# Norm gain before, norm root after: the S5 input projection of a hybrid layer on one Trainium2 core

## The chip, the cores and the metric

The kernel runs on one core of a Trainium2 chip. Its time is the device time of one execution in microseconds (us); a kernel's time is the median over its runs. A profiled execution lasts from the program's start to its end; its span, from the first to the last instruction, is a little shorter. The engines are named as in the profile: PE multiplies matrices (PEld is its loading of weights), DVE and ACT work elementwise, POOL helps them, and SP issues most of the transfers (DMAs). An engine works through its instructions in order: if one waits, everything behind it on that engine waits too.

## The reference

One layer of a trunk with 1024 channels and 1024 time steps. What matters here is its start:

```python
def rms_norm(x, g):
    y = xf * lax.rsqrt(jnp.mean(xf * xf, axis=-1, keepdims=True) + NORM_EPS)
    return y.astype(x.dtype) * g

h = rms_norm(x, norm_mix_pre[l])
proj = h @ w_in[l]
p_rwkv = proj[..., :N_RWKV_COLS]
u_s5 = proj[..., N_RWKV_COLS:N_RWKV_COLS + S5_WIDTH]      # 512 columns
gates = jax.nn.sigmoid(proj[..., N_RWKV_COLS + S5_WIDTH:] + b_gate[l])
# s5_branch: a diagonal complex state space over u_s5: b_bar = (exp(lam*dt) - 1) / lam * b,
# an associative scan over time, Re(c s) + d u, then gelu and a sigmoid gate
o_s5 = s5_branch(u_s5, s5_a_re[l], s5_a_im[l], ...)
```

The RWKV branch, the merge of both branches, the output projection and a gated MLP follow.

## The kernel before

Tiles are 128 channels by 512 time steps; a half (`th` 0 or 1) is one 512 of the 1024 time steps, and `k` counts the eight groups of 128 channels. A product in full precision is three matmuls (`mm3_steps`, L172 to L174): each operand is split into a rounded high part and the rest, and high×high, high×low and low×high are added in PSUM. So a weight tile `wf` becomes `wh` (ACT, L156) and `wl` (DVE, L157), and a normed tile `x` becomes `hh` (ACT, L226) and `hl` (`hsplit`, L227: for odd `k` on POOL, for even `k` on DVE).

The front of the kernel is written in `front_half`. `norm(th)` squares the eight tiles on ACT (L955), adds the squares in pairs on DVE (L956), sums each pair over channels with four matmuls of one column (`sumsq`, L245), takes the inverse root on DVE (L265, and L131 to L139), spreads it over the partitions with four transposes (`spread`, L271), copies it to SBUF as `rbc` (ACT, L964), and multiplies each tile in place by the norm's weight and the root (DVE, L967), after which it is split. `s5_in` then makes the S5 inputs: for each half, 8 k × 4 output tiles b × 3 matmuls, 96 in all, evicted by an ACT copy that reverses and permutes the time steps (L1073), stored to HBM (`US`) and loaded again in another order as `u8` (`load_u8`). After that `s5_setup` works the 32-column parameters of S5 out on DVE in some 115 small operations (L320 to L475).

From there two lanes run beside a filler. `s5_tables` (L508 to L575 on DVE, then `abs` and two sines on ACT, L576 to L578) makes the tables of one batch b of 8 groups; `s5_batch` multiplies `u8` by them (PE L598), rotates (DVE L600 to L602), scans (L605), rotates back (L607, L608; L608's is the last) and makes the batch's outputs (PE L613 to L615). The filler is the other columns of the input projection: `mix_in` (the RWKV columns, evicted on ACT L977 and shifted on DVE L978) and `gate_tiles` (evicted on ACT L1013, where a table of the activation may have to be loaded).

PE's order is written by hand. `drive` keeps a planned time `now`: each step of a lane names its cost and how long it must rest before its next step (`T_TAB0` before the first batch's tables come on PE, `T_TRIG`, `T_SCAN`), and matmuls of the filler are set in between to fill these rests. On the chip this order is fixed: PE waits at a step of S5 if its tables or scans aren't there, whatever stands behind it. The other engines' orders are set by the scheduler, by priority (`HPN` before `HP`) and the time at which it expects operands. Filler matmuls come out of four PSUM tiles (`gm`); an eviction that is late stops PE when the fifth is wanted.

At the start the `vecs` (norm weights, biases) and the constants `csts` are loaded on POOL's queue, the raw S5 parameters (`ls`, `lr`, `li`) on SP's (L314 to L316).

## Time and profile before

| | |
|---|---|
| median of 3 runs | 1551.08 us (1547.18 to 1552.98) |
| the profiled execution's own time | 1552.89 us |
| its span | 1551.1 us |
| mean granted PE clock | 0.972 |
| PE busy | 1460.4 us |
| DVE busy | 1081.2 us |
| ACT busy | 687.0 us |
| first S5 input matmul on PE | 25.57 us |
| first operation of the first S5 tables on DVE | 78.96 us |
| PE's matmuls of the first S5 outputs that need the scans (L614) | 144.15 us |

The page gives each engine's busy share. The waits on PE are listed by what ended them; the timeline gives a row's start in us from the span's start, its length, and in brackets the idle time before it. A row with x2 or x4 joins so many instructions.

### The profile page before, as it was taken

The page shows a single profiled execution, that of the slowest core. Times are in us where ns is not written, and L with a number is a line of the kernel's source. Part 1 is how long each engine was busy: PE and PEld are TensorE (multiplying, and loading weights), DVE is VectorE, ACT ScalarE, POOL GpSimd, SP SyncE. Part 2 cuts the span into 40 slices and gives each one's busy share as a digit, 9 for nine tenths or more (in the row PEclk, how much of TensorE's full clock was granted, in tenths as well). Part 3 has the DMA queues.
Part 4 walks back from the last instruction along what each step waited for, and adds up shares of the span by engine and source line. Part 5 has one row for each costly group of instructions (what it writes and reads, how often), then busy time and mean ns, then how long its engine had stood idle before and what let it go on. Part 6 is the DMA issues. An engine that isn't in the chain of part 4 may idle for free.

```text
span 1551.1 us, 24273 instructions
## 1 busy us (share of the span) xinstructions
PE 1460.4 (94%) x9332; PEld 1194.8 (77%) x9332; DVE 1081.2 (70%) x1733; ACT 687.0 (44%) x1069; POOL 161.1 (10%) x180
## 2 busy tenths in 40 slices
...
GB/s 208 41 203 118 93 127 100 196 115 113 153 44 107 153 190 143 144 69 94 255 245 161 153 144 137 103 82 82 82 84 88 87 82 203 334 149 134 241 59 108
DMA packets 131107, 210.45 MB, mean 136 GB/s; under 512 B 37696, under 2 KB 43840, under 8 KB 130992
## 3 DMA queue, kind: packets, MB, share of 16 engines
...
## 4 chain that ended last, share of the span: by engine, by line
PE 69%; DVE 12%; DMA 8%; issue 5%; ACT 4%; POOL 1%; SPq 0%; DVEq 0%; ACTq 0%; POOLq 0%
PE gm L172 8%; PE gm L173 8%; PE gm L174 7%; PE rp L1382 4%; PE rp L1383 4%; PE rp L1384 4%; DMA st<-in_w_down_dram 2%; PE mm L1383 2%; PE mm L1382 2%; PE mm L1384 2%; PE ch L172 2%; PE ch L173 2%; PE ch L174 2%; PE d L1557 2%; PE d L1556 2%
## 5 line engine op out<-in xcount | busy, mean ns | idle before, releaser
L172 PE MATMUL gm<-hh,wh 128*128 128x512 f32 x688 | 284.7, 414 | 14.2 <-DVE hl L1118 8.8
L173 PE MATMUL gm<-hl,wh 128*128 128x512 f32 x688 | 273.4, 397 | 0.2 <-DVE hl L227 0.2
L174 PE MATMUL gm<-hh,wl 128*128 128x512 f32 x656 | 260.0, 396 | 0.0
L157 DVE TENSOR_TENSOR wl<-wf,wh 128x512 fp32r<-128x512 f32 x175 | 123.1, 705 | 116.1 <-ACT wh L156 108.1
L156 ACT CAST wh<-wf 128x512 fp32r<-128x512 f32 x179 | 110.5, 619 | 209.6 <-PE gm L173 129.4
L172 PEld LDWEIGHTS gm<-hh,wh 128*128 128x128 f32 x688 | 132.2, 192 | 49.0 <-DVE hl L1118 10.9
L173 PEld LDWEIGHTS gm<-hl,wh 128*128 128x128 f32 x688 | 132.3, 192 | 26.3 <-issue 1.0
L174 PEld LDWEIGHTS gm<-hh,wl 128*128 128x128 f32 x656 | 125.6, 191 | 27.5
L1557 PE MATMUL d<-xl,wh 128*128 128x512 f32 x308 | 120.2, 390 | 3.5 <-DVE xl L227 3.5
L1556 PE MATMUL d<-xh,wh 128*128 128x512 f32 x308 | 120.1, 390 | 2.1 <-ACT xh L226 2.1
L1558 PE MATMUL d<-xh,wl 128*128 128x512 f32 x308 | 119.9, 389 | 0.0
L1382 PE MATMUL rp<-t,h 128*128 128x512 f32 x216 | 84.4, 391 | 1.4 <-ACT p L1396 1.4
L1384 PE MATMUL rp<-t,l 128*128 128x512 f32 x216 | 84.2, 390 | 0.5 <-DVE l L227 0.5
L1383 PE MATMUL rp<-t,h 128*128 128x512 f32 x216 | 84.1, 389 | 0.0
L1557 PEld LDWEIGHTS d<-xl,wh 128*128 128x128 f32 x308 | 57.8, 188 | 16.5 <-DVE xl L227 4.8
L1556 PEld LDWEIGHTS d<-xh,wh 128*128 128x128 f32 x308 | 57.8, 188 | 14.5 <-ACT xh L226 2.5
L1558 PEld LDWEIGHTS d<-xh,wl 128*128 128x128 f32 x308 | 57.8, 188 | 12.0
L226 ACT CAST h<-r 128x1024 fp32r<-128x1024 f32 x34 | 35.8, 1054 | 61.1 <-PE rp L1383 32.5
L227 DVE TENSOR_TENSOR l<-r,h 128x1024 fp32r<-128x1024 f32 x34 | 41.6, 1224 | 29.2 <-ACT h L226 27.7
L1403 DVE SCALAR_TENSOR_TENSOR y<-zv,vecs,y 128x1023 f32<-128x1023 f32 (+1 forms) x36 | 46.1, 1280 | 8.5 <-ACT y L1401 8.5
L1382 PEld LDWEIGHTS rp<-t,h 128*128 128x128 f32 x216 | 40.5, 188 | 10.8 <-ACT p L1396 2.2
L1384 PEld LDWEIGHTS rp<-t,l 128*128 128x128 f32 x216 | 40.6, 188 | 9.4 <-DVE l L227 1.0
...
## 6 DMA issues: line engine op xcount, KB each, us to landing
...
wf<-in_w_in_dram SPq DMA_DIRECT2D x68, 256.0 KB, 3.0
st<-in_w_down_dram SPq DMA_DIRECT2D x55, 256.0 KB, 4.3
st<-ACT SPq DMA_DIRECT2D x44, 256.0 KB, 4.4
wf<-in_w_up_dram SPq DMA_DIRECT2D x36, 256.0 KB, 2.7
...
GT<-ev SPq DMA_DIRECT2D x32, 256.0 KB, 2.4
wf<-in_w_br_dram SPq DMA_DIRECT2D x32, 256.0 KB, 3.4
```

Source lines behind the costliest of these rows:

```text
L156: nc.scalar.copy(h[:, :n], f[:, :n])
L157: nc.vector.tensor_tensor(l[:, :n], f[:, :n], h[:, :n].bitcast(F32), ALU.subtract)
L172: mm(ps, a, xh[k], start=k == 0, stop=False)
L173: mm(ps, a, xl[k], start=False, stop=False)
L174: mm(ps, b, xh[k], start=False, stop=k == n - 1)
L1382: mm(ps, wh[:, c], xh, start=first and k == 0, stop=False, skip_group_check=True)
L1383: mm(ps, wh[:, c], xl, start=False, stop=False, skip_group_check=True)
L1384: mm(ps, wl[:, c], xh, start=False, stop=k == 3, skip_group_check=True)
L1403: V.scalar_tensor_tensor(y[:, lag:], z[:, 0:1024 - lag], self.vec(nme, i), y[:, lag:], ALU.mult, ALU.add)
L1556: mm(ps, wh[:, c], xh[:, x], start=start, stop=False, skip_group_check=True)
L1557: mm(ps, wh[:, c], xl[:, x], start=False, stop=False, skip_group_check=True)
L1558: mm(ps, wl[:, c], xh[:, x], start=False, stop=stop, skip_group_check=True)
```

## The change

`norm`, `load_x` and `s5_in` are replaced by one function, `start`. The S5 inputs are no longer made from the normed h, but from x times the norm's weight (`gained`: the high part on ACT, the rest on DVE), which needs no root; the root of each time step is multiplied in when the product is evicted (`evict`), on DVE instead of ACT. The normed and split h is still made for the filler (`scaled`), all of its low parts on DVE; half 0's stand between the S5 matmuls of half 1, half 1's behind them. The squares are not added in pairs: each tile's are summed on PE, 16 tiles in place of 8 pairs, between the S5 matmuls. `vecs` and the raw S5 parameters are asked for first, on ACT's queue; the weights of S5 come in half tiles between x's tiles, three of the four through the `u8` tiles as a staging place; the larger part of the constants and the batch weights come behind all of x. `s5_setup` is emitted ahead of the filler. The planner's rest before the first tables is 25 instead of 20.

```diff
--- before.py
+++ after.py
@@ -272,13 +272,16 @@
                                      self.cst("ident"))
 
 
-    def setup(self):
+    def setup(self, xp):
         nc = self.nc
         self.vecs = self.const.tile([128, NVEC], F32, name="vecs")
         self.csts = self.const.tile([128, NCST], F32, name="csts")
+        nc.scalar.dma_start(self.vecs, self.a["vec"])
+        raw = xp.tile([128, 4, 32], F32, name="s5raw")
+        self.s5raw = [raw[:, i] for i in range(3)]
+        for t, x in zip(self.s5raw, (self.a["s5_ls"], self.a["s5_a"][0], self.a["s5_a"][1])):
+            nc.scalar.dma_start(t, x)
         nc.gpsimd.dma_start(self.csts[:, 0:128], self.a["cst"][:, 0:128])
-        nc.gpsimd.dma_start(self.vecs, self.a["vec"])
-        nc.gpsimd.dma_start(self.csts[:, 128:NCST], self.a["cst"][:, 128:NCST])
         self.ones1 = self.const.tile([128, 1], F32, name="ones1")
         nc.gpsimd.memset(self.ones1, 1.0)
         self.last = self.const.tile([128, 14], F32, name="last")
@@ -286,6 +289,8 @@
         self.hpi = self.const.tile([128, 1], F32, name="hpi")
         nc.gpsimd.memset(self.hpi, math.pi / 2)
 
+    def setup_vecs(self):
+        nc = self.nc
         o, n = VEC["mu"]
         self.mu1 = self.const.tile([128, n], F32, name="mu1")
         nc.vector.tensor_scalar(self.mu1, self.vecs[:, o:o + n], -1.0, 1.0, ALU.mult, ALU.add)
@@ -310,10 +315,7 @@
         with self.tc.tile_pool(name="s5tmp", bufs=1) as pool:
             def sm(n=32, dt=F32):
                 return pool.tile([128, n], dt, name=self.nm("sm"))
-            lr, li, ls = sm(), sm(), sm()
-            nc.sync.dma_start(ls, a["s5_ls"])
-            nc.sync.dma_start(lr, a["s5_a"][0])
-            nc.sync.dma_start(li, a["s5_a"][1])
+            ls, lr, li = self.s5raw
 
             def ts(x, s1, s2, o0, o1=None, out=None, n=32):
                 y = out if out is not None else sm(n)
@@ -936,38 +938,124 @@
-    def load_x(self, th, pool):
...
+    def start(self, pool):
+        nc, V, A, G = self.nc, self.nc.vector, self.nc.scalar, self.nc.gpsimd
+        raw = {}
+        xs = [[pool.tile([128, 512], F32, name=self.nm("x"), tag="x", bufs=16) for k in range(NK)] for th in range(2)]
+        w = [([], []) for b in range(4)]
+        def load_x(th, k):
+            nc.sync.dma_start(xs[th][k], self.a["x"][k * 128:k * 128 + 128, th * 512:th * 512 + 512])
+        def load_w(b, i):
+            if b < 3:
+                f = self.u8[b].rearrange("p g n -> p (g n)")[:, i * 512:i * 512 + 512]
+            else:
+                f = self.wp.tile([128, 512], F32, tag="wf", name=self.nm("wf"), bufs=NWF)
+            raw[b, i] = f
+            nc.sync.dma_start(f, self.a["w_in"][14 + b][:, i * 512:i * 512 + 512])
+        def split_w(b, i):
+            own = pool if b > 1 else self.wp
+            h = own.tile([128, 512], F32R, tag="wh", name=self.nm("wh"), bufs=4 if b > 1 else NWH)
+            l = self.lx() if b > 1 else own.tile([128, 512], F32R, tag="wl", name=self.nm("wl"), bufs=NWL)
+            self.split(h, l, raw[b, i])
+            w[b][0].append(h)
+            w[b][1].append(l)
+        def gained(th, k):
+            hi, lo = self.pair(th, k)
+            g = self.vec("g_mix_pre", k)
+            A.activation(hi, xs[th][k], AF.Identity, scale=g)
+            V.scalar_tensor_tensor(lo, xs[th][k], g, hi.bitcast(F32), ALU.mult, ALU.subtract)
+            return hi, lo
+        def square(th, k):
+            sq = pool.tile([128, 512], F32, tag="sq", name=self.nm("sq"), bufs=4)
+            A.activation(sq, xs[th][k], AF.Square)
+            sqs[th].append(sq)
+        def summed(th, *ks):
+            for k in ks:
+                self.sumsq(sums[th][:, 0:512], sqs[th][k], k == 0)
+        def root(th):
+            return self.rstd(sums[th], 1e-6, 1.0 / D)
+        def scales(th, y):
+            bc = sums[th][:, 512:1024]
+            self.spread(bc, y)
+            r = pool.tile([128, 512], F32, tag="rbc", name=self.nm("rbc"), bufs=2)
+            A.copy(r, bc)
+            return r
+        def scaled(th, k):
+            x = xs[th][k]
+            V.scalar_tensor_tensor(x, x, self.vec("g_mix_pre", k), rbc[th], ALU.mult, ALU.mult)
+            self.h[th][k] = self.hsplit(x, k, self.hp[th], eng=V)
+        def evict(th, b, ps):
+            y = self.ev((128, 8, 64))
+            p, r = [x.rearrange("p (n j) -> p n j", j=8)[:, :, ::-1] for x in (ps, rbc[th])]
+            V.tensor_tensor(y.rearrange("p i n -> p n i"), p, r, ALU.mult)
+            nc.sync.dma_start(self.US[b].rearrange("i c g n -> (c g) i n")[:, :, th * 64:th * 64 + 64], y)
+            if self.stored is not None:
+                self.load_u8(self.stored)
+                self.stored = None
+            if th:
+                self.stored = b
+        load_x(0, 0)
+        for i in range(2):
+            for b in range(4):
+                load_w(b, i)
+            for k in range(4 * i, 4 * i + 4):
+                if k:
+                    load_x(0, k)
         for k in range(NK):
...
+            load_x(1, k)
+        nc.sync.dma_start(self.csts[:, 128:NCST], self.a["cst"][:, 128:NCST])
+        self.s5_load(0)
+        self.s5_load(1)
+        self.h = [[None] * NK, [None] * NK]
+        sums, sqs, rbc = [self.chk() for th in range(2)], [[], []], [None, None]
+        g = [[], []]
         for k in range(NK):
...
+            g[0].append(gained(0, k))
+            if k % 4 == 0:
+                for b in range(4):
+                    split_w(b, k // 4)
+            square(0, k)
+        for th in range(2):
+            ps = [self.gmp() for b in range(4)]
+            for k in range(NK):
+                for b in range(4):
+                    a, l = [x[k // 4][:, k % 4 * 128:k % 4 * 128 + 128] for x in w[b]]
+                    hi, lo = g[th][k]
+                    nc.tensor.matmul(ps[b], a, hi, start=k == 0, stop=False)
+                    nc.tensor.matmul(ps[b], a, lo, start=False, stop=False)
+                    nc.tensor.matmul(ps[b], l, hi, start=False, stop=k == NK - 1)
+                    if k == NK - 1:
+                        evict(th, b, ps[b])
+                if th:
+                    summed(1, *{0: (4, 5), 1: (6, 7)}.get(k, ()))
+                else:
+                    summed(0, *{4: (4, 5), 5: (6, 7)}.get(k, (k,) if k < 4 else ()))
+                if k == (1 if th else 5):
+                    y = root(th)
+                if k == (3 if th else 6):
+                    rbc[th] = scales(th, y)
+                if th:
+                    scaled(0, k)
+                elif k >= 4:
+                    for q in (2 * k - 8, 2 * k - 7):
+                        g[1].append(gained(1, q))
+                        square(1, q)
+                    if k > 5:
+                        summed(1, 2 * k - 12, 2 * k - 11)
+        for k in range(NK):
+            scaled(1, k)
-    def norm(self, th, xs, pool):
...
@@ -1056,27 +1144,6 @@
-    def s5_in(self, pool):
...
@@ -1763,21 +1830,15 @@
             self.u8 = [u8p.tile([128, 8, 128], F32, name=f"u8_{b}") for b in range(4)]
             with tc.tile_pool(name="xp", bufs=1) as xp:
                 with tc.high_priority(HPN):
-                    xs = [self.load_x(0, xp)]
-                    self.setup()
+                    self.setup(xp)
                     self.s5w = {}
-                    self.s5_load(0)
-                    self.s5_load(1)
-                    for _ in self.norm(0, xs[0], xp):
-                        pass
-                    xs.append(self.load_x(1, xp))
-                self.fill = [self.s5_in(xp), self.mix_in()] + [self.gate_tiles(m) for m in range(14)] + [
+                    self.start(xp)
+                    self.setup_vecs()
+                with tc.high_priority(HP):
+                    self.s5_setup()
+                self.fill = [self.mix_in()] + [self.gate_tiles(m) for m in range(14)] + [
                     self.merge_loads(), self.gate_tiles(14, 15)]
                 self.outs, self.yr = 0, []
-                self.drive([(HPN, self.norm(1, xs[1], xp))])
-                self.drain(lambda: self.stored == 3)
-                with tc.high_priority(HP):
-                    self.s5_setup()
             with tc.tile_pool(name="s5p", bufs=1) as self.s5p:
                 self.s5d = [{} for _ in range(4)]
                 self.tabs = self.s5_done = -1
@@ -1857,12 +1918,11 @@
                 self.fill += [self.merge(mg), self.outproj(0, mg, self.mx0)]
 
 
-T_US, T_TAB0, T_TAB, T_TRIG, T_SCAN = 5.0, 20.0, 20.0, 12.0, 13.0
+T_US, T_TAB0, T_TAB, T_TRIG, T_SCAN = 5.0, 25.0, 20.0, 12.0, 13.0
 T_LD, T_SQ, T_LT = 6.0, 3.0, 3.5
 NEVA = 4
 T_KN, T_BK, T_GR, T_NF, T_MT, T_INV, T_LV, T_CH = 7.0, 7.0, 4.0, 5.0, 8.0, 43.0, 1.0, 0.8
 T_LN, T_LE = 32.0, 20.0
-T_X = 8.0
```

Lines behind this move: the tables and batches of S5 by 2 (L600 becomes L602, L608 L610, L614 L616), the filler's evictions by 88 (L977 becomes L1065, L1013 L1101). The S5 input matmuls are L1036 to L1038 now, and the weights' low parts there are L227.

DVE at the start, where the norm's weights `vecs` have come; `sm` are S5's small parameters, `hl` the low part of x times the weight. Before:

```order
L301 TENSOR_SCALAR ka_h<-vecs 128x4
L302 TENSOR_SCALAR ka_222<-vecs 128x4
L157 TENSOR_TENSOR wl_356<-wf_357,wh_355 128x512
L157 TENSOR_TENSOR wl_362<-wf_363,wh_361 128x512
L956 TENSOR_TENSOR sq_242<-sq_242,sq_243 128x512
L956 TENSOR_TENSOR sq_251<-sq_251,sq_252 128x512
```

Now, from the 23rd instruction:

```order
L330 TENSOR_TENSOR sm_943<-sm_939,sm_941 128x32
L335 SCALAR_TENSOR_TENSOR sm_829<-sm_827,sm_821 128x32
L408 RECIPROCAL sm_945<-sm_943 128x32
L971 SCALAR_TENSOR_TENSOR hl_260<-x_198,vecs,hh_259 128x512
L227 TENSOR_TENSOR wl_264<-u_0_177,wh_263 128x512
L227 TENSOR_TENSOR wl_268<-u_1_178,wh_267 128x512
L227 TENSOR_TENSOR lx_272<-u_2_179,wh_271 128x512
L227 TENSOR_TENSOR lx_276<-wf_218,wh_275 128x512
```

Eighteen of S5's small operations have moved ahead of the first large one, and PE's second matmul needs `hl_260`.

ACT at the sines of the first batch (`t` are S5's tables). Before:

```order
L576 ACTIVATE t_289_1227<-t_291_1229 128x1024
L156 CAST wh_1660<-wf_1662 128x512
L977 ACTIVATE ev_1462<-gm_1339,mu_211 128x512
L1013 ACTIVATE ev_1483<-gm_1419,hb_a_217 128x512
L1013 ACTIVATE ev_1499<-gm_1486,hb_a_217 128x512
L577 ACT_TABLE_LOAD
L577 ACTIVATE t_290_1228<-t_291_1229 128x1024
L578 ACTIVATE t_289_1227<-t_289_1227,hpi 128x1024
```

Now:

```order
L578 ACTIVATE t_314_1333<-t_316_1335 128x1024
L1065 ACTIVATE ev_1603<-gm_1524,mu_796 128x512
L1101 ACTIVATE ev_1615<-gm_1596,hb_a_802 128x512
L579 ACT_TABLE_LOAD
L579 ACTIVATE t_315_1334<-t_316_1335 128x1024
L1101 ACT_TABLE_LOAD
L1101 ACTIVATE ev_1631<-gm_1618,hb_a_802 128x512
L580 ACT_TABLE_LOAD
L580 ACTIVATE t_314_1333<-t_314_1333,hpi 128x1024
```

An eviction of the gates has moved between the two sines, with a table load on either side.

DVE at the end of the first batch's scans. Before, the second batch's phases began behind L608, and their last operation L575 stood here:

```order
L574 TENSOR_SCALAR t_368_1586<-t_370_1588 128x1024
L575 TENSOR_TENSOR t_370_1588<-t_370_1588,t_368_1586 128x1024
L157 TENSOR_TENSOR wl_1999<-wf_2000,wh_1998 128x512
L978 SCALAR_TENSOR_TENSOR ev_1809<-gm_1751,vecs,ev_1809 128x511
L982 SCALAR_TENSOR_TENSOR ev_1809<-last,vecs,ev_1809 128x1
L600 TENSOR_TENSOR t_390_1695<-chk_1764,t_368_1586 128x1024
```

Now four of the five operations before them stand among the first batch's scans (L607) and rotations back (L609, L610):

```order
L571 TENSOR_TENSOR t_395_1692<-csts,s5fh 128x1024
L607 SCALAR_TENSOR_TENSOR t_342_1458<-s5rho,t_343_1460 128x127
L572 TENSOR_SCALAR t_393_1690<-t_395_1692 128x1024
L607 SCALAR_TENSOR_TENSOR t_342_1458<-s5rho,t_343_1460 128x127
L573 TENSOR_TENSOR t_395_1692<-t_395_1692,t_393_1690 128x1024
L607 SCALAR_TENSOR_TENSOR t_342_1458<-s5rho,t_343_1460 128x127 x2
L609 TENSOR_TENSOR t_343_1460<-t_342_1458,t_315_1334 128x1024
L574 TENSOR_TENSOR t_394_1691<-csts,s5fl 128x1024
L610 TENSOR_TENSOR t_342_1458<-t_342_1458,t_314_1333 128x1024
L575 TENSOR_TENSOR t_395_1692<-t_395_1692,t_394_1691 128x1024
L576 TENSOR_SCALAR t_393_1690<-t_395_1692 128x1024
L577 TENSOR_TENSOR t_395_1692<-t_395_1692,t_393_1690 128x1024
```

The second batch's phases now end (L577) directly behind the first batch's L610, with 19 instructions between L577 and the second batch's L602 instead of 3.

44 lines of the change are left out of this document (removed).

## The prediction

> **What bounds the kernel now.** I read the page's head first, then the list of PE's waits over the first 310 us, then PE's timeline there, because the change ends in the first 80 us and can only push what follows.
>
> ```profile
> span 1551.1 us, 24273 instructions
> PE 1460.4 (94%) x9332; PEld 1194.8 (77%) x9332; DVE 1081.2 (70%) x1733; ACT 687.0 (44%) x1069; POOL 161.1 (10%) x180
> PE 69%; DVE 12%; DMA 8%; issue 5%; ACT 4%; POOL 1%; SPq 0%; DVEq 0%; ACTq 0%; POOLq 0%
> ```
>
> The span is 1551.1 us, the execution 1552.89, and the median of the runs 1551.08. PE is busy for 94% and carries 69% of the chain that ended last. So a gain must be either less work on PE or fewer waits in front of PE. These are the waits that matter here (the last row is from DVE's list):
>
> ```profile
> PE chk L614 <- DVE t L608: 5.1, 2, 4.0
> PE chk L544 <- DVE t L600: 2.1, 1, 2.1
> PE gm L172 <- ACT ev L1013: 1.9, 1, 1.9
> PE chk L553 <- DVE t L601: 0.7, 1, 0.7
> ...
> DVE t L600 <- ACT t L578: 10.2, 2, 6.5
> ```
>
> Each row has the total, the number of waits and the longest. Three of PE's four are S5's lane: PE comes to its tables or scans before DVE has them, and DVE waits for ACT's sines. So S5's lane on DVE bounds PE as well, from 130 to 190 us. What bounds the start is in PE's own timeline:
>
> ```profile
> 8.05 0.17 DVE L291 TENSOR_SCALAR mu<-vecs 128x14 f32<-128x14 f32 x1 [8.05 <-DMA vecs<-in_vec_dram]
> ...
> 25.57 0.80 PE L172 MATMUL gm<-hh,wh 128*128 128x512 f32 x1 [2.23 <-ACT hh L226]
> ...
> 30.61 0.63 PE L173 MATMUL gm<-hl,wh 128*128 128x512 f32 x1
> 31.04 0.51 PE L174 MATMUL gm<-hh,lx 128*128 128x512 f32 x1
> ...
> 36.60 0.39 PE L174 MATMUL gm<-hh,lx 128*128 128x512 f32 x1
> 36.83 0.95 PE L245 MATMUL chk<-ones,sq 128*128 128x1 f32 x8
> 37.64 0.49 PE L172 MATMUL gm<-hh,wh 128*128 128x512 f32 x1
> ...
> 84.01 0.69 ACT L977 ACTIVATE ev<-gm,mu 128x512 f32<-128x512 f32 x1 [2.82 <-PE gm L174]
> ```
>
> The reader is to see three things. PE's first real matmul comes at 25.57, behind the whole norm of half 0. Up to about 31 us a matmul takes 0.43 us (30.61 to 31.04), later 0.23 (36.60 to 36.83); a sum of squares of one tile takes 0.81 (36.83 to 37.64). And the first tile of the filler is evicted at 84.01; its 24 matmuls and about 0.6 us for the last one's end lie in front, so the S5 inputs end on PE at 84.0 - 0.6 - 24 x 0.2265 = 78.0.
>
> **Part 1: PE's start.** The S5 inputs need no root now, so PE can begin as soon as the norm's weights, the first tile of x and the first weights are split. `vecs` moves from POOL's queue to the front of ACT's.
>
> ```profile
> vecs<-in_vec_dram POOLq DMA_DIRECT2D x1, 135.0 KB, 6.0
> wf<-in_w_in_dram SPq DMA_DIRECT2D x4, 256.0 KB, 3.5
> ```
>
> On POOL's queue it took 6.0 us and DVE had it at 8.05; the first weights on SP's queue took 3.5. I take the value of the rows it is now nearest to, first on its queue like the weights: `vecs` at about 4, bounds 3.5 and 8. Behind it stand 7 setup operations and 18 of S5's small ones ahead of the first `hl` (the order shows it), some 2.5 us together, with the raw parameters' landing between them: first `hl` at about 7, PE's first matmul there as well, and the four low parts of the first weights, 0.69 each, until about 10. The Trainium skill speaks against this part: DMA: Bandwidth & Descriptors, in its specifications, gives a first byte after about 1 us on GpSimd's path and 0.6 on SP's and ACT's, so that the queue alone would be worth 0.4 us and `vecs` would be there at 7.6; by that, the estimate of the sum below would be 3.6 us worse. The two rows differ by 2.5 us, though they are of different transfers.
>
> PE's work then: half 0 has 96 matmuls x 0.2265 = 21.7, twelve sums of squares (eight of its own, four of half 1) x 0.81 = 9.7 and a spread of 0.9, 32.3 together. At first the matmuls are slow as before from 25.57 to 31.04: 5.5 us at half rate lose 2.7; waits for the splits I put at 0.8. So half 0 ends at 7.0 + 32.3 + 3.5 = 42.8. Half 1: 21.7 + four sums 3.2 + 0.9 = 25.8. In it I expect one wait of 2: the spread of half 1 needs the inverse root, and DVE has two weight splits of the filler ahead of it, whose high parts wait for the buffers that these very matmuls free. End: 42.8 + 25.8 + 2.0 + 0.2 = 70.8 instead of 78.0, a gain of **7.2**. The eight sums more on PE (6.5 us) are within it. Before, POOL made eight low parts; DVE, not POOL, makes them now, so POOL's part is no cover any more.
>
> **Part 2: DVE up to S5's first tables.** This decides whether the 7.2 us are kept.
>
> ```profile
> 0.00:25.00 25.00, 8.24 (x36) 7.70 (x36) 9.81 (x29) 11.55 (x19) 2.29 (x12) 1.00 0.73 229
> 25.00:50.00 25.00, 24.19 (x110) 19.98 (x111) 23.96 (x103) 10.87 (x21) 6.41 (x4) 1.00 0.30 95
> 50.00:75.00 25.00, 23.84 (x105) 18.87 (x104) 20.27 (x64) 10.72 (x18) 5.89 (x4) 1.00 0.27 64
> ...
> 125.00:150.00 25.00, 21.94 (x124) 18.37 (x123) 19.24 (x32) 14.14 (x18) 0.95 (x2) 0.93 0.39 114
> ...
> 175.00:200.00 25.00, 18.19 (x108) 15.75 (x107) 21.10 (x30) 10.23 (x15) 0.32 (x2) 0.93 0.25 69
> ```
>
> ```profile
> L967 DVE SCALAR_TENSOR_TENSOR x<-x,vecs,rbc 128x512 f32<-128x512 f32 x16 | 14.4, 936 | 1.8 <-ACT rbc L964 1.8
> L227 DVE TENSOR_TENSOR hl<-x,hh 128x512 fp32r<-128x512 f32 x8 | 7.5, 936 | 0.1
> L956 DVE TENSOR_TENSOR sq<-sq,sq 128x512 f32<-128x512 f32 x8 | 6.6, 824 | 1.7 <-ACT sq L955 1.6
> L157 DVE TENSOR_TENSOR wl<-wf,wh 128x512 fp32r<-128x512 f32 x8 | 5.3, 686 | 8.9 <-PE gm L173 6.4 <-ACT wh L156 2.5
> ...
> L1098 DVE TENSOR_TENSOR hl<-ld,hh 128x512 fp32r<-128x512 f32 x4 | 4.2, 1061 | 0.0
> ```
>
> The windows' third pair is DVE. Until the first tables DVE was busy 9.81 + 23.96 + 20.27 + 1.4 (two splits behind 75 us) = 55.4. The large operations are 14.4 + 7.5 + 6.6 + 12 splits x 0.69 = 36.8, so the small ones take 18.6. Now the large ones are 12 splits and 16 `hl` of h at 0.69, 16 products x0.74 (the mean of 936 ns comes from the times when POOL worked beside DVE; alone they take 743 at the median), 16 new `hl` of x times the weight at 0.74, and 8 evictions. No row shows a DVE eviction with reversed, permuted columns; it ends between 0.69 (a plain operation) and 1.11 (ACT's old eviction), and I take 1.06 from L1098, which is a DVE operation on the same permuted tile. 28 x 0.69 + 32 x 0.74 + 8 x 1.06 = 51.5, with the small ones 70.1: **14.7 us more** than before. It can begin at about 4 us instead of 8; with some 4 us of waits (parameters and x at the start, the sums of half 1, the evictions for PE's last matmuls) the tables begin at 4 + 70.1 + 4 = 78 instead of 78.96. With evictions at 0.69 and no waits it would be 71, with `vecs` at 8 and twice the waits 86. So DVE, which had slack under PE's late start, has none left: PE is ready 7.2 us earlier, S5's tables only 1.
>
> **Part 3: S5's first batch.**
>
> ```profile
> 78.96 0.28 DVE L508 TENSOR_TENSOR sml<-s_b,s5q 128x128 f32<-128x128 f32 x1
> ...
> 127.03 1.06 ACT L576 ACTIVATE t<-t 128x1024 f32<-128x1024 f32 x1 [8.94 <-DVE t L575]
> ...
> 133.78 1.22 DVE L600 TENSOR_TENSOR t<-chk,t 128x1024 f32<-128x1024 f32 x1 [3.67 <-ACT t L578]
> ...
> 142.79 1.22 DVE L608 TENSOR_TENSOR t<-t,t 128x1024 f32<-128x1024 f32 x1
> 144.15 0.46 PE L614 MATMUL chk<-t,ca 128*128 128x128 f32 x2 [1.12 <-DVE t L608]
> ...
> 145.17 1.21 DVE L569 TENSOR_TENSOR t<-csts,s5fh 128x1024 f32<-128x1024 f32 x1
> ...
> 149.41 1.23 DVE L573 TENSOR_TENSOR t<-t,t 128x1024 f32<-128x1024 f32 x1
> ```
>
> From the first table operation to the phases' end took 48.1 us (78.96 to 127.03). The same rows stand there now and three small ones more: 78 + 48.9 = 126.9. From there to L600's start were 6.75, with the two sines, two evictions and one table load between. Now ACT has two more loads and one more eviction between the sines but two fewer operations ahead, and what it does ahead of the last sine's end is: 1.06 + 2 x 0.69 + 1.28 + 1.06 + 1.28 + 0.69 + 1.28 + 1.06 = 9.1 (the sines taken as long as the operation at 127.03, the evictions as long as the one at 84.01). These are the rows of a like stretch, in the second batch:
>
> ```profile
> 172.58 1.28 ACT L994 ACT_TABLE_LOAD   x1
> 173.88 0.63 ACT L994 ACTIVATE ev<-ev 128x512 f32<-128x512 f32 x1
> 174.53 1.28 ACT L578 ACT_TABLE_LOAD   x1
> ```
>
> A load takes 1.28 and the next instruction starts 1.30 behind its start. The Trainium skill (ScalarE: Activation LUTs, What ACT_TABLE_LOAD costs) says 1.28 us and a drain of 1.38 for each switch, 2.66; here no drain is seen (172.58 to 173.88), so the measurement decides; by the page the two loads more would cost an estimated 2.8 us beyond my sum.
>
> L600 to L608's end took 10.2 (133.78 to 144.01). Among the scans stand now four of the second batch's five phase operations, which took 145.17 to 150.64 for all five, so about 4.3, and two weight splits and some small ones, 2.3: 16.8. So the scans' result comes at 126.9 + 9.1 + 16.8 = 152.8 instead of 144.0. PE stands there, in its fixed order, with 18 filler matmuls (4.1 us, `T_TAB0`) more behind it than before; without waits it would be there at 143.0 - 7.2 + 4.1 = 139.9, so it waits 13 instead of 1.1. Everything before this point on PE, the 7.2 us, the wait of 1.9 for the gates' eviction and its slow matmuls, is swallowed. PE is 8.8 us late, with 4.1 us of work more done: **+4.7**.
>
> **Part 4: behind it.**
>
> ```profile
> 187.13 0.46 PE L614 MATMUL chk<-t,ca 128*128 128x128 f32 x2 [4.00 <-DVE t L608]
> ...
> 309.45 0.43 PE L716 MATMUL cz<-ar,bk 64*64 64x128 f32 x2 [1.44 <-DVE gr L719]
> ```
>
> The second batch's scans came at 187.0, 43 behind the first's, of which 6.5 were DVE's wait for the second sines and 6.6 are the operations that now stand ahead. So they come 30 behind: 183. PE's way between the two took 43.0 with waits of 2.1, 0.7 and 4.0, so 36.2: it arrives at 189 and does not wait. These waits go, 6.8, and so does the slow stretch behind the last: the granted clock of 175 to 200 us is 0.93, 0.07 x 25 = 1.75 lost. **-8.5**. Behind the wait of 13 us comes such a stretch instead (the window of 125 to 150 has one too, also 0.93; that one was swallowed): **+1.75**. The later batches did not wait and are 6 us from it. Last, the 4.1 us of filler done early are missing as cover where RWKV starts; PE waited there already 1.44 (309.45), so it can cost from 0 to 4.1; I take 1.5, since the other waits there are not in the list: **+1.5**.
>
> Sum: 4.7 - 8.5 + 1.75 + 1.5 = -0.6. Against the profiled execution 1552.3, against the median **1550.5**: no change. A measurement of this kernel can tell about 0.5%, 7.8 us.
>
> **The rivals.** *Faster:* DVE is no bound, and PE keeps its start. For it speaks that DVE's large operations get rid of POOL's disturbance, and that the waits of 4 us are my reading of an order, not a row. With plain evictions and no waits the tables begin at 71, the scans end at 146, 7 us sooner than in my sum: -7.6, 1543.5. If DVE is never late, PE keeps all of -7.2, -1.1 - 1.9 - 1.75 of the first batch's waits, -8.5, against 1.5: -19 at most, 1532, but that needs tables before 65, 6 us sooner than DVE's own work, begun at 4 us with plain evictions, allows. So 1538 to 1543. Against it: the 14.7 us more on DVE are counted from instructions that stand there.
>
> *Slower:* DVE is later than 86 at the tables. One mechanism is enough: `vecs` and the raw parameters land late. They stand ahead of the first low part on DVE, and behind that stands all of DVE's work; a microsecond there goes one to one to the scans and to PE. At 8 us for `vecs` it is +4, which is still no change (1554.5); it decides from 8.4 us on, 12.4 us for the landing, to which the small-packet parameters or a queue full of x and weights would have to push it; in that case 1559 to 1563. For it speaks that in the trace of before `vecs` took 6.0 us while x was loading, and that x tiles 4 to 7 stand behind a weight of the filler on SP's queue, which waits for a buffer that DVE frees.
>
> *The change doesn't do what it says:* PE starts no earlier than 11 since the first low parts wait; the gain of 7.2 becomes 3. As PE waits for the scans anyway, the time moves only by what DVE loses: 1550 to 1554, within no change.
>
> *The second batch keeps its waits* of 8.5: its margin of 6 us would have to be lost on DVE or ACT. Then 1559.
>
> **How the numbers follow.** My forecast with the third rival, no change: 0.47. Faster: 0.27, since one of DVE's terms at its lower end suffices. Slower: 0.26, 0.18 for the late tables and 0.08 for the second batch. The range: below, plain evictions, half the waits and no loss at RWKV, with a little of the faster rival, 1540; above, the late parameters and part of the second batch's waits, 1561.
>
> **What will show it.** PE's first S5 matmul at 6 to 8, its last at about 70 to 71; DVE's first table operation at 76 to 80; L610's end near 153, and at PE's L616 of the first batch a wait of 10 us or more for DVE; at the second batch none. The forecast is wrong if the tables begin before 72 or after 86, if the wait at L616 is under 5, or if the second batch's waits stay.

## The result, and the profile after

The changed kernel takes 1556.37 us (median of 12 runs, 1551.88 to 1563.10), the kernel before beside it 1549.17 (12 runs, 1546.93 to 1552.98). The ratio is 1.0047, with a 95% interval of 1.0033 to 1.0062: slower by 7.2 us. That lies inside the 0.5% that was called no change and inside the range of 1540 to 1561, but the forecast had a difference of -0.6 us, and the interval does not reach it.

The head of the page of the changed kernel. The execution shown here was the slowest of the twelve, 1563.1 us:

```profile
span 1561.2 us, 24423 instructions
PE 1468.7 (94%) x9396; PEld 1202.4 (77%) x9396; DVE 1090.5 (70%) x1757; ACT 693.1 (44%) x1079; POOL 149.7 (10%) x170
```

PE is as full as before, 94%. PE's waits over the first 330 us of the same execution (total, number, longest):

```profile
PE chk L616 <- POOL kpad L552: 9.3, 1, 9.3
...
PE chk L546 <- DVE t L602: 4.4, 1, 4.4
PE cz L718 <- DVE gr L721: 3.9, 1, 3.9
PE gm L172 <- DVE last L1068: 3.7, 1, 3.7
PE chk L271 <- DVE rsy L139: 2.2, 2, 1.9
```

The wait at L616, 9.3, is the forecast one for the first batch's scans; the POOL operation named in its row had long been done, and the second trace below names DVE's L610. With the 4.4 at L546, for the same lane, it makes 13.7, where 13 were forecast. The second batch's waits are not in the list, also as forecast. The 3.9 and the 3.7 lie where RWKV starts, behind S5; before, the waits there were 1.4 and 1.9. The timeline of the same execution (start, duration, engine, line; the wait in brackets):

```profile
6.97 0.80 PE L1036 MATMUL gm<-hh,wh 128*128 128x512 f32 x1 [6.97 <-ACT wh L226]
...
78.17 0.39 PE L1038 MATMUL gm<-hh,lx 128*128 128x512 f32 x1
85.74 0.29 DVE L510 TENSOR_TENSOR sml<-s_b,s5q 128x128 f32<-128x128 f32 x1
134.66 1.06 ACT L578 ACTIVATE t<-t 128x1024 f32<-128x1024 f32 x1 [4.24 <-DVE t L577]
143.74 1.22 DVE L602 TENSOR_TENSOR t<-chk,t 128x1024 f32<-128x1024 f32 x1 [6.54 <-ACT t L580]
159.14 1.22 DVE L610 TENSOR_TENSOR t<-t,t 128x1024 f32<-128x1024 f32 x1
160.51 0.77 PE L616 MATMUL chk<-t,ca 128*128 128x128 f32 x2 [9.33 <-POOL kpad L552]
```

PE starts its S5 inputs at 6.97 instead of 25.57, and yet ends them at 78.4 (78.17 and one issue), no earlier than before. DVE's first table operation comes at 85.74; 78 was forecast. All behind it keeps the forecast's distances: 48.9 to the phases' end, 9.1 to L602, 16.6 from there to L610's end.

A second trace of the same kernel (execution of 1560.25 us, span 1558.4) lies nearer to its median difference, +7.3 against the span before. Its rows are used where terms are counted. Its timeline:

```profile
74.13 0.39 PE L1038 MATMUL gm<-hh,lx 128*128 128x512 f32 x1
...
81.89 0.29 DVE L510 TENSOR_TENSOR sml<-s_b,s5q 128x128 f32<-128x128 f32 x1
...
156.71 0.77 PE L616 MATMUL chk<-t,ca 128*128 128x128 f32 x2 [8.98 <-DVE t L610]
...
263.97 0.39 PE L616 MATMUL chk<-t,ca 128*128 128x128 f32 x2
...
316.76 0.43 PE L718 MATMUL cz<-ar,bk 64*64 64x128 f32 x2 [3.88 <-DVE gr L721]
```

These points cut the program into three stages: up to the first batch's L616 (L614 before), from there to the first L616 of S5's last batch (called S5's last outputs below), and from there to RWKV's second group (the 309.45 of the prediction). Stage by stage, the kernel before (length; then busy time and number of records of PE, PEld, DVE, ACT, POOL; then granted clock, DMA share, GB/s):

```profile
0.00:144.15 144.15, 122.36 (x571) 101.04 (x572) 114.34 (x292) 70.50 (x108) 25.97 (x31) 0.99 0.49 148
144.15:258.68 114.53, 107.72 (x609) 93.42 (x610) 88.46 (x128) 44.01 (x60) 4.95 (x7) 0.99 0.35 106
258.68:309.45 50.77, 47.48 (x293) 39.57 (x291) 32.93 (x47) 20.64 (x35) 26.58 (x23) 0.97 0.52 171
```

The changed kernel, second trace:

```profile
0.00:156.71 156.71, 132.22 (x653) 109.04 (x654) 129.01 (x329) 78.70 (x123) 17.41 (x22) 0.95 0.50 149
156.71:263.97 107.26, 107.26 (x610) 93.40 (x611) 82.10 (x117) 42.27 (x56) 2.74 (x6) 0.98 0.31 95
263.97:316.76 52.79, 43.67 (x274) 36.11 (x272) 33.70 (x45) 19.60 (x34) 26.63 (x24) 0.97 0.49 163
```

| stage | forecast | measured | off by |
|---|---|---|---|
| to the first batch's L616 | +8.8 (4.7, and 4.1 of filler done early) | +12.6 | +3.8 |
| S5's batches | -6.75 (-8.5 + 1.75) | -7.3 | -0.5 |
| to RWKV's second group | -2.6 (-4.1 of filler, +1.5) | +2.0 | +4.6 |
| behind it | 0 | 0.0 (7.3 at RWKV, 7.3 at the end) | 0 |
| sum | -0.6 | +7.3 | +7.9 |

The 0.0 in the fourth row is this execution's: the first trace of the change is 11.4 us late at RWKV and 10.1 at its end, a third one 9.7 and 5.8.

So the question has two parts: why S5's tables came at 82 to 86 instead of 78, and where the filler that PE had done early went, which should have shortened the stage in front of RWKV. The last row shows the second already: 19 records and 3.8 us of work fewer on PE, but 9.1 us of idle time in it (52.79 - 43.67) instead of 3.3. Three waits make the difference of 5.8 us: PE's first wait there, in front of the filler (3.7 instead of 1.9), a second one there (1.6, new) and the one at RWKV's products (3.9 instead of 1.4). The rows for the first of them, in the second trace:

```profile
273.17 1.64 DVE L630 TENSOR_SCALAR rkb<-csts,vecs 128x128 f32<-128x128 f32 x4 [10.35 <-issue]
275.68 0.47 PE L172 MATMUL gm<-hh,wh 128*128 128x512 f32 x1 [3.67 <-DVE last L1068]
```

L630 is the first operation of RWKV's setup. DVE stands idle for 10.35 us in front of it, and the filler's eviction, which ends with L1068, comes behind it in DVE's order. In the kernel before, DVE did an eviction of the filler ahead of that operation (at 266.17), and PE waited 1.85.

### The profile page after: what moved, and what is told of

The parts are those of the page before. It is cut to its first block, busy times and chain, and to the rows that moved or that the text cites. A ratio compares the mean times of both kernels' runs of the same rounds, so it can differ in the third digit from the quotient of the medians.

```text
span 1561.2 us, 24423 instructions
## 1 busy us (share of the span) xinstructions
PE 1468.7 (94%) x9396; PEld 1202.4 (77%) x9396; DVE 1090.5 (70%) x1757; ACT 693.1 (44%) x1079; POOL 149.7 (10%) x170
## 5 line engine op out<-in xcount | busy, mean ns | idle before, releaser
L172 PE MATMUL gm<-hh,wh 128*128 128x512 f32 x624 | 257.6, 413 | 14.9 <-DVE hl L1185 9.1
L173 PE MATMUL gm<-hl,wh 128*128 128x512 f32 x624 | 246.0, 394 | 0.0
L174 PE MATMUL gm<-hh,wl 128*128 128x512 f32 x624 | 245.8, 394 | 0.0
L156 ACT CAST wh<-wf 128x512 fp32r<-128x512 f32 x171 | 105.7, 619 | 193.4 <-PE gm L173 105.0
L172 PEld LDWEIGHTS gm<-hh,wh 128*128 128x128 f32 x624 | 118.7, 190 | 46.4 <-DVE hl L1185 11.1
L174 PEld LDWEIGHTS gm<-hh,wl 128*128 128x128 f32 x624 | 118.6, 190 | 26.2
L173 PEld LDWEIGHTS gm<-hl,wh 128*128 128x128 f32 x624 | 119.0, 191 | 23.3 <-issue 1.2
L1450 PE MATMUL rp<-t,h 128*128 128x512 f32 x216 | 84.1, 389 | 0.0
L227 DVE TENSOR_TENSOR l<-r,h 128x1024 fp32r<-128x1024 f32 x34 | 41.6, 1225 | 29.2 <-ACT h L226 27.7
```

The costliest lines, as they stand in the source:

```text
L156: nc.scalar.copy(h[:, :n], f[:, :n])
L172: mm(ps, a, xh[k], start=k == 0, stop=False)
L173: mm(ps, a, xl[k], start=False, stop=False)
L174: mm(ps, b, xh[k], start=False, stop=k == n - 1)
L227: (eng or self.nc.vector).tensor_tensor(lo, x, hi.bitcast(F32), ALU.subtract)
L1450: mm(ps, wh[:, c], xl, start=False, stop=False, skip_group_check=True)
```

## The experiments

The theory (A in the expectations): S5's tables come late, their distance to the end is fixed, and what makes them late stands in front of them, on the way over PE's last S5 inputs and DVE. The rivals: PE's own added work, the eight sums of squares more (B); and the filler taken early by `T_TAB0` = 25, which is missing later (D). The table has the places of every trace in us (S is DVE's first table operation). Ratios are to the kernel before, run on the same chip, with their 95% intervals; the rows' places come from one execution each.

| kernel | S | first L616 | S5's last outputs | RWKV's 2nd group | span | ratio |
|---|---|---|---|---|---|---|
| before | 79.0 | 144.2 | 258.7 | 309.5 | 1551.1 | 1 |
| change | 85.7 | 160.5 | 268.5 | 320.9 | 1561.2 | 1.0047 [1.0033, 1.0062] |
| change, 2nd trace | 81.9 | 156.7 | 264.0 | 316.8 | 1558.4 | 1.0050 [1.0033, 1.0067] |
| change, 3rd trace | 82.8 | 158.1 | 265.9 | 319.1 | 1556.9 | 1.0030 [1.0012, 1.0048] |
| sq6 | 85.8 | 161.5 | 269.7 | 321.3 | 1562.8 | 1.0079 [1.0054, 1.0104] |
| evict_plain | 74.9 | 140.1 | 253.7 | 307.2 | 1549.4 | 1.0006 [0.9983, 1.0028] |
| tab20 | 83.4 | 148.2 | 264.4 | 318.6 | 1562.0 | 1.0067 [1.0042, 1.0092] |
| pool_split | 80.6 | 150.4 | 264.9 | 317.0 | 1556.3 | 1.0060 [1.0037, 1.0084] |
| early_roots | 83.3 | 155.8 | 263.8 | 316.2 | 1553.0 | 1.0020 [1.0007, 1.0033] |
| pair_sums | 85.3 | 159.6 | 266.9 | 318.9 | 1559.4 | 1.0066 [1.0049, 1.0083] |
| half1_rooted | 86.1 | 154.1 | 267.0 | 319.3 | 1563.5 | 1.0093 [1.0072, 1.0114] |
| before_tables_late | 79.2 | 152.6 | 266.8 | 318.8 | 1559.7 | 1.0033 [1.0014, 1.0052] |
| evict_two_steps | 82.0 | 154.3 | 262.8 | 315.5 | 1551.8 | 0.9998 [0.9981, 1.0014] |
| two_steps_again | 79.9 | 152.2 | 260.6 | 312.9 | 1548.3 | 1.0012 [0.9996, 1.0028] |
| old_queues | 80.8 | 152.4 | 265.5 | 318.0 | 1558.2 | 1.0034 [1.0014, 1.0055] |
| early_two_steps | 81.3 | 149.9 | 263.3 | 314.7 | 1554.7 | 1.0035 [1.0017, 1.0053] |
| before_tab25 | 80.3 | 149.5 | 264.3 | 317.6 | 1569.6 | 1.0112 [1.0095, 1.0129] |

**sq6.** The squares get six buffers instead of four, since ACT waited 8.7 us in all for PE to free them.

```diff
-            sq = pool.tile([128, 512], F32, tag="sq", name=self.nm("sq"), bufs=4)
+            sq = pool.tile([128, 512], F32, tag="sq", name=self.nm("sq"), bufs=6)
```

> The changed kernel with six buffers for the squares in place of four. In its trace ACT waits 1.8, 2.4, 1.2, 0.6 us for a square's buffer that PE's sums free, and DVE then waits 6.3 us for the high parts behind them on ACT. Theory A (S5's first tables on DVE set the end; DVE waits at the two inverse roots for PE's sums): the 6.3 us fall to 2 or less, but DVE then waits longer at the roots, since PE's sums stand where they stood. The first table operation stays at 85.7 within 1.5 us, the time at 1556 within 1.5. Rival C (the short buffers themselves make DVE late): first table operation 4 to 5 us earlier, time 1551 to 1553.

The tables stayed at 85.8, within the 81.9 to 85.7 of the change itself: the buffers are not what holds them. The time, 1563.14 against 1553.82, came out above what was expected; this trace has a granted clock of only 0.86 in the window of 25 to 50 us.

**evict_plain.** ACT evicts the S5 inputs, without the multiplication by the root.

```diff
-            V.tensor_tensor(y.rearrange("p i n -> p n i"), p, r, ALU.mult)
+            A.copy(y.rearrange("p i n -> p n i"), p)
```

> The changed kernel with the S5 inputs evicted by a plain ACT copy, as before the change; the root is left out of them, so S5's inputs are scaled wrongly. DVE loses eight operations of 1.07 us ahead of the tables. Theory A: the four of half 1 come off one to one; the four of half 0 stand before DVE's wait of 4.2 us for half 1's sums and give most of theirs back there. First table operation at 80.5 to 82 in place of 85.7, PE's wait at the first batch's L616 4 to 5 us shorter, time 1551 to 1553. Rival B (the loss is PE's own: the eight sums more and the two stretches at half clock behind sums): PE's start is unchanged, so the time stays at 1555 to 1557.

The tables came at 74.85, earlier than expected, since two things went at once: DVE's eight evictions, and the slow stretch on PE. Against the second trace of the change, half 1's sums reach DVE 2.1 us earlier (53.45 instead of 55.51), and behind them DVE needs 21.4 us to the tables instead of 26.4. The windows of 25 to 75 us in this trace:

```profile
25.00:50.00 25.00, 24.69 (x151) 21.51 (x151) 18.48 (x79) 19.72 (x35) 0.00 (x0) 1.00 0.37 98
50.00:75.00 25.00, 25.00 (x122) 20.94 (x121) 20.20 (x62) 12.05 (x18) 0.12 (x1) 1.00 0.22 59
```

The granted clock is 1.00 in both, and PE ends the S5 inputs at 70.2, close to the 70.8 of the prediction. The clock alone does not give that: tab20 has 1.00 in both windows too and ends them at 75.9. There the slow start lasts for 19 matmuls instead of 8, and PE waits 2.1 us for the first low part and 1.9 for half 1's root; here these waits are 1.4 and nothing. But the time is only level with before, and the stages say where the gain went. The same kernel:

```profile
0.00:140.10 140.10, 128.63 (x654) 107.37 (x654) 116.24 (x312) 82.16 (x129) 14.58 (x21) 0.99 0.53 158
140.10:253.70 113.60, 108.12 (x609) 94.01 (x610) 87.69 (x126) 39.21 (x54) 5.63 (x7) 0.97 0.35 100
253.70:307.15 53.45, 44.95 (x274) 37.05 (x272) 33.87 (x45) 19.84 (x34) 26.06 (x24) 0.92 0.50 161
```

S5 is done 5.0 us earlier than in the kernel before, RWKV's second group comes only 2.3 earlier: the last stage takes 53.45 instead of 50.77, with 8.5 us of idle time on PE in it.

**tab20.** `T_TAB0` back at 20, all else as in the change.

```diff
-T_US, T_TAB0, T_TAB, T_TRIG, T_SCAN = 5.0, 25.0, 20.0, 12.0, 13.0
+T_US, T_TAB0, T_TAB, T_TRIG, T_SCAN = 5.0, 20.0, 20.0, 12.0, 13.0
```

> The changed kernel with the planner's rest before the first tables back at 20 instead of 25, so that 18 filler matmuls (4.1 us) that PE did ahead of S5's steps come behind them. Theory A: the scans come when they came (160 us), PE waits 4 us longer in front of the first batch and has 4.1 us more left; of this the RWKV start gives back what the missing cover costs, 0 to 4 us: time 1556 to 1560. Rival D (the larger rest is what costs, by leaving RWKV's start without cover: waits of 3.7 and 3.9 us there against 1.9 and 1.4 before): those two waits fall to 2 and 1.5 and the time falls to 1552 to 1554.

The last stage of this trace:

```profile
264.40:318.60 54.20, 47.01 (x294) 38.78 (x293) 34.88 (x47) 20.34 (x35) 25.17 (x23) 1.00 0.51 161
```

The filler is there again (294 records, as in the kernel before), and the stage is longer still, 54.2, with 7.2 us of idle time instead of 3.3. The two waits that D named did fall, from 3.9 to 2.2 and from 3.7 to 1.9, but another of 2.8 came between them, and the time is not better, 1.0067. So filler done early is not by itself what lengthens the stage, and rival D falls as the cause of the loss.

**pool_split.** POOL makes every second low part of h.

```diff
-            self.h[th][k] = self.hsplit(x, k, self.hp[th], eng=V)
+            self.h[th][k] = self.hsplit(x, k, self.hp[th], eng=G if k % 2 else V)
```

> The changed kernel with the low parts of h for odd k on POOL again, as before the change; eight subtractions of 0.69 leave DVE. Theory A: DVE gains 5.5 us of work but loses some where POOL works beside it (before, DVE operations beside POOL took up to 1.78 in place of 0.68 to 0.74): first table operation 0 to 4 us earlier, time 1552 to 1557. Rival B (loss on PE): unchanged, 1555 to 1558.

The tables come at 80.6, 1.3 to 5.1 us ahead of the change's three traces, yet the ratio of 1.0060 is no better than the change's. POOL takes 1773 ns for each of the eight, against 686 on DVE.

**after_again.** The changed kernel once more, unchanged.

> The changed kernel unaltered, as the yardstick on the chip of the next three. Its profiled execution took 1563.1 us against a median of 1556.4, so a second profile shows which of its readings hold: theory A expects the first table operation at 85.7 and the scans at 160 within 1.5 us again, no wait at the second batch's L616, and two waits of 3.5 to 4 us at the start of RWKV; the rest of the difference to the median would then lie behind 330 us. If the tables begin below 83 this time, the lateness that I read off the first profile is partly that execution's.

The ratio repeats, 1.0050. S differs by 3.9 us between the two traces, and so does PE's end of the S5 inputs (78.4 and 74.4). The slow stretch in this trace follows the sums and the spread of half 0's root, with 0.3 us of idle time ahead of the spread and none behind it. PE's timeline there:

```profile
40.41 0.41 PE L1037 MATMUL gm<-hl,wh 128*128 128x512 f32 x1
40.63 0.61 PE L1038 MATMUL gm<-hh,wl 128*128 128x512 f32 x1
41.04 0.63 PE L1036 MATMUL gm<-hh,wh 128*128 128x512 f32 x1
```

From 40.63 on one matmul takes 0.42 instead of 0.23, until 44.0. The first trace has two such stretches (15 slow matmuls against 8), and its slow start lasts for 19 matmuls instead of 11.

**early_roots.** Sums and roots one step of the loop earlier, half 0's scaled tiles earlier too, and six buffers for the squares.

```diff
-            sq = pool.tile([128, 512], F32, tag="sq", name=self.nm("sq"), bufs=4)
+            sq = pool.tile([128, 512], F32, tag="sq", name=self.nm("sq"), bufs=6)
...
-                    summed(1, *{0: (4, 5), 1: (6, 7)}.get(k, ()))
+                    summed(1, *{0: (6, 7)}.get(k, ()))
...
-                    summed(0, *{4: (4, 5), 5: (6, 7)}.get(k, (k,) if k < 4 else ()))
-                if k == (1 if th else 5):
+                    summed(0, *{3: (3, 4), 4: (5, 6, 7)}.get(k, (k,) if k < 3 else ()))
+                if k == (0 if th else 4):
                     y = root(th)
-                if k == (3 if th else 6):
+                if k == (2 if th else 5):
                     rbc[th] = scales(th, y)
...
```

> The changed kernel with the same work, but PE's sums of squares earlier between the matmuls, so that both roots come one step of k (about 3.6 us) earlier, with six buffers for the squares. Theory A (DVE idles for the sums and then has the scaling of h, the evictions and the splits left): root of half 0 at 31 to 33 instead of 37.2, root of half 1 at 50 to 53 instead of 57.9; DVE's waits at the two roots fall from 6.6 to 4 or less; first table operation at 79 to 82, time 1550 to 1554. If DVE's lateness is its amount of work, not the waits: tables at 84 to 86, time unchanged at 1555 to 1558.

The time came out as expected, 1.0020, but S at 83.3 did not: DVE's wait for the sums stays (5.6 us), and a wait of 5.3 for PE stands before the first eviction. So an earlier root did not bring the tables forward, and why this version is somewhat faster isn't told by its tables.

**pair_sums.** DVE adds the squares in pairs, and PE sums four tiles of each half instead of eight.

```diff
             sqs[th].append(sq)
+            if k % 2:
+                V.tensor_tensor(sqs[th][k - 1], sqs[th][k - 1], sq, ALU.add)
...
             for k in ks:
-                self.sumsq(sums[th][:, 0:512], sqs[th][k], k == 0)
+                if k % 2:
+                    self.sumsq(sums[th][:, 0:512], sqs[th][k - 1], k == 1)
```

> The changed kernel with the squares added in pairs on DVE again, as before the change, so PE sums 8 pairs in place of 16 tiles: PE loses 6.5 us of work ahead of the S5 inputs' end, DVE gets 8 x 0.69 = 5.5 us more. Rival B (PE's own work and the half-clock stretches behind sums cost): the S5 inputs end at 65 to 67 instead of 73.6 and the time falls by 4 to 7 us, to 1549 to 1552. Theory A: part of the 5.5 us falls into DVE's idle time before 44 us; first table operation at 84 to 89, time 1554 to 1560, though PE is early.

PE ends the S5 inputs at 69.8, 4.6 us sooner than in the second trace, and it gains nothing: the tables come at 85.3, the ratio is 1.0066. PE's waits show the work that DVE got in exchange:

```profile
PE chk L616 <- DVE t L610: 9.6, 1, 9.6
PE chk L555 <- DVE ca L535: 7.2, 1, 7.2
```

Half 1's sums reach DVE at 49.4, but from there to the tables DVE needs 35.9 us instead of 26.4. Rival B falls: PE's added sums alone are not the price, and the sooner PE's end is, the more DVE itself is the bound.

**half1_rooted.** Half 1 goes into S5 from h, scaled by the root ahead of the product, as before the change; half 0 as in the change.

```diff
-                    hi, lo = g[th][k]
+                    hi, lo = self.h[1][k] if th else g[0][k]
...
-            V.tensor_tensor(y.rearrange("p i n -> p n i"), p, r, ALU.mult)
+            if th:
+                A.copy(y.rearrange("p i n -> p n i"), p)
+            else:
+                V.tensor_tensor(y.rearrange("p i n -> p n i"), p, r, ALU.mult)
...
```

> A version of the change for half 0 alone: half 0 goes without the root as in the change, half 1 from the normed h, whose root is ready by then, since PE sums all squares among half 0's matmuls (six buffers for squares). DVE loses eight products with the weight (8 x 0.74) and four evictions (4 x 1.07), 10.2 us; PE has the same work. Theory A: first table operation at 72 to 77, scans of the first batch at or before PE, time as with plain evictions or a little less: 1546 to 1551. Rival B: 1555 to 1557, or later if PE waits between the halves for the first normed tiles (0 to 4 us).

The work that this takes off DVE (eight low parts, four evictions) was expected to bring S to 72 to 77. It came at 86.1, for DVE waited. DVE's waits up to there:

```profile
DVE rv L265 <- PE chk L245: 9.6, 2, 8.4
DVE wl L157 <- PE gm L1046: 7.4, 1, 7.4
DVE sm L330 <- ACT sm L390: 7.3, 1, 7.3
```

All sums now stand together in half 0, and PE ran at a granted clock of 0.78 from 25 to 50 us. PE ended the S5 inputs at 85.5, and the tables followed: the wait of 7.4, for the buffer of a weight's low part that PE's S5 matmuls free, ended at 84.1.

**before_tables_late.** The kernel before, with seven multiplications by 1.0 on DVE in the first batch's tables, 5.2 us.

```diff
         V.tensor_tensor(w, w, wt, ALU.add)
+        for _ in range(7 if b == 0 else 0):
+            V.tensor_scalar(w, w, 1.0, None, ALU.mult)
```

> The kernel before, with seven multiplications by one (128x1024, some 0.61 us each, 4.3 us together) among the DVE operations of the first batch's tables; nothing else differs. Theory A, sharpened by the eight traces so far (from the first table operation to PE's last outputs of S5 took 179 to 184 us in all of them, whether PE waited at the first batch, at the second or at neither): S5's end comes 4 to 5 us later, RWKV's first loads with it, and the time is 3 to 6 us longer. If PE bounds the front and S5's lane has slack (PE waited only 1.1 us at the first batch's scans): 0 to 1.5 us longer, most of it in that wait.

PE's waits up to 330 us:

```profile
PE chk L546 <- DVE t L525: 8.3, 1, 8.3
PE chk L616 <- DVE t L610: 4.0, 1, 4.0
PE cz L718 <- DVE gr L721: 2.7, 1, 2.7
```

A new wait of 8.3 for the tables, and a ratio of 1.0033, 5.1 us (2.2 to 8.1), for 5.2 us on DVE. Nothing else of the change is in this kernel, so late tables alone cost time at the end, of the size of what they are late. That it is one to one, a single trace does not show: in it S5's last outputs are 8.1 us later, not 5.2. Its last stage takes 52.0 instead of 50.8.

**evict_two_steps.** DVE multiplies in PSUM in plain order, ACT copies into the permuted order.

```diff
-            p, r = [x.rearrange("p (n j) -> p n j", j=8)[:, :, ::-1] for x in (ps, rbc[th])]
-            V.tensor_tensor(y.rearrange("p i n -> p n i"), p, r, ALU.mult)
+            V.tensor_tensor(ps, ps, rbc[th], ALU.mult)
+            A.copy(y.rearrange("p i n -> p n i"), ps.rearrange("p (n j) -> p n j", j=8)[:, :, ::-1])
```

> The changed kernel with each eviction of the S5 inputs in two steps: DVE multiplies by the root in place in PSUM, in plain order, and ACT copies with the permutation, as before the change. If DVE's 1.07 us is the price of the permuted order, DVE's part falls to 0.6 to 0.7, 3.2 us less in all; half 0's share falls into the wait for half 1's sums. Theory A: first table operation 1.5 to 3 us earlier than the 81.9 of the second look, time 1 to 3 us below the changed kernel's (ratio to the kernel before 1.003 to 1.0045). If the product from PSUM is slow in any order: no change in either.

DVE's group of the eight evictions, here:

```profile
L1000 DVE TENSOR_TENSOR gm<-gm,rbc 128x512 f32<-128x512 f32 x8 | 5.4, 698 | 2.2 <-PE gm L1038 2.2
```

and in the change:

```profile
L1001 DVE TENSOR_TENSOR ev<-gm,rbc 128x512 f32<-128x512 f32 x8 | 7.9, 1075 | 2.0 <-PE gm L1038 2.0
```

One eviction takes 698 ns instead of 1075. The ratio is 0.9998, level with before. **two_steps_again** is the same kernel on another chip.

> The changed kernel with evictions in two steps, beside the changed kernel on one chip. In the first run its ratio to the kernel before was 0.9998, 0.5% below the changed kernel's of another chip job, while its first table operation (82.0) stood where the changed kernel's second look has it (81.9). Theory A from that profile: S5's end 1 us earlier only, so it should be 0 to 0.15% faster than the changed kernel here. If shorter evictions are worth more than the profile shows: 0.3 to 0.5% faster, level with the kernel before.

The ratio is 1.0012, and the changed kernel on that chip, **after_third**, has 1.0030.

> The changed kernel unaltered, as the yardstick for the two runs beside it: 1.004 to 1.006 of the kernel before, as in both comparisons so far. In the profile the first table operation stands at 82 to 86, later by 1.7 us for each stretch of PE at half clock behind sums of squares ahead of 70 us; S5's last outputs 181 to 184 us behind it.

So two steps are the best of the versions, level with before in both series, though on this chip its interval and the change's overlap. In neither trace is RWKV's second group as early as in the kernel before (315.5 and 312.9 against 309.5); both regain most of it or all in the 1235 to 1236 us behind it (1241.7 before; 1237.8 to 1241.6 in the three traces of the change). The second of these traces is of the fastest of its twelve runs. What gives them that, the runs don't tell.

**old_queues.** `vecs` on POOL's queue and the raw parameters on SP's, as before the change.

```diff
-        nc.scalar.dma_start(self.vecs, self.a["vec"])
...
-            nc.scalar.dma_start(t, x)
+            nc.sync.dma_start(t, x)
         nc.gpsimd.dma_start(self.csts[:, 0:128], self.a["cst"][:, 0:128])
+        nc.gpsimd.dma_start(self.vecs, self.a["vec"])
```

> The changed kernel with one part undone: vecs is asked for on POOL's queue and the raw S5 parameters on SP's, ahead of x, as POOL's queue had vecs before the change. vecs then lands at about 8 instead of 4.5 and x's first tile about 1 us later; PE's first S5 matmul comes at 10 to 11 instead of 7. Theory A: PE's sums, both roots and with them the tables come 2 to 4 us later, time 2 to 4 us above the changed kernel's (ratio 1.006 to 1.0075). If the wait for parameters is hidden by the later waits for x and the sums: 1.0045 to 1.0055.

`vecs` was expected at about 8 and came at 5.3:

```profile
5.32 0.18 DVE L296 TENSOR_SCALAR mu<-vecs 128x14 f32<-128x14 f32 x1 [1.85 <-DMA vecs<-in_vec_dram]
```

PE starts at 8.5 instead of 7.0, S is 80.8 where 2 to 4 us more were expected, the ratio 1.0034: the queues' part of the change has no worth that these runs can tell.

**early_two_steps.** The edits of early_roots and evict_two_steps together.

> The two changes that took time off together: earlier sums and roots, and the eviction in two steps. Theory A: first table operation at 80 to 82, S5's last outputs on PE at 261 to 263, ratio to the kernel before 1.000 to 1.002; it beats the kernel before only if the tables begin ahead of 79.0. If DVE waits for the eviction of half 0 in order (5.3 us in the run with early roots) whatever it costs: as that run, 1.002.

Expected were 1.000 to 1.002, measured 1.0035 (1.0017 to 1.0053). The small gains of the two do not add, and a wait of 5.1 us at the second batch's scans is back.

**before_tab25.** The kernel before with `T_TAB0` at 25.

```diff
-T_US, T_TAB0, T_TAB, T_TRIG, T_SCAN = 5.0, 20.0, 20.0, 12.0, 13.0
+T_US, T_TAB0, T_TAB, T_TRIG, T_SCAN = 5.0, 25.0, 20.0, 12.0, 13.0
```

> The kernel before with one number of the change, the planner's rest before the first tables 25 instead of 20, so that 18 to 24 filler matmuls (4 to 5.5 us) come ahead of S5's steps on PE and are missing ahead of RWKV's. My forecast counted such matmuls as work done early (4.1 us off the path, less 0 to 4.1 of cover). By that: 0 to 4 us faster. Theory A (S5's lane on DVE sets its own end, 179 to 184 us behind its first operation, and RWKV's second group of chunk products came 51 to 54 us behind that end in every trace, however much filler stood between): S5's last outputs at 258 to 261, RWKV as before or up to 3 us later, time the same to 3 us slower (1.000 to 1.002).

It is slower by 1.1%, of which some 8 us stand at RWKV's second group (1.3 of them from a later start of this execution) and 10 arise behind, where the planner's order changed too. PE has 22 records more in its first stage and none fewer in the last (295 against 293). So this doesn't isolate the 18 matmuls, and it gives no sign that filler taken early is worth anything.

## Why the prediction was right and wrong

**Right.** PE's first S5 matmul (6.97, forecast 7). `vecs`: DVE's wait for it ended at 4.5, forecast 4; but the reason given, the queue, was wrong, and the number luck. old_queues has `vecs` on POOL's queue, behind a part of the constants as before, and there by 5.3: the queue, with the place on it, is worth 0.8 us of the 3.5; the rest is left to the other changes to the loads. So the estimate of 7.6 from the Trainium skill (DMA: Bandwidth & Descriptors, specifications) was off as a time, but the small worth that it gave the queue, 0.4 us, is nearer to these runs than the 2.5 read from the two rows. PE's wait for half 1's root (1.9, forecast 2). DVE's new eviction (1075 ns, forecast 1060). From the first table operation to the last sine's start 48.9, as forecast. The stretch between the sines: ACT's rows in the changed kernel,

```profile
136.89 1.28 ACT L579 ACT_TABLE_LOAD   x1
138.18 1.06 ACT L579 ACTIVATE t<-t 128x1024 f32<-128x1024 f32 x1
139.26 1.28 ACT L1101 ACT_TABLE_LOAD   x1
140.56 0.69 ACT L1101 ACTIVATE ev<-gm,hb_a 128x512 f32<-128x512 f32 x1
141.26 1.28 ACT L580 ACT_TABLE_LOAD   x1
```

give 9.1 from 134.66 to L602, as forecast: the instruction behind a load starts 1.28 to 1.30 after the load's start. The drain that the Trainium skill gives for it (ScalarE: Activation LUTs, What ACT_TABLE_LOAD costs) is not seen here either. The scans (16.6, forecast 16.8), PE's waits for the first batch (13.4 to 13.7 in two places, forecast 13 in one), and the second batch without any. So Part 3's distances held, from a start that was 3.9 us later, and of Part 4 the -8.5 and +1.75, which measured -7.3.

**Wrong, first: PE's S5 inputs in Part 1, half 0's end at 42.8 and the whole at 70.8, by 3.4 and 3.6 us; and the "some 4 us of waits" in Part 2's 78 for the tables.** From 6.95 to 74.36 PE took 67.4 us in the second trace, where 63.8 were summed. Worked out from the starts in its timeline: eight matmuls at half rate, behind the sums and the spread, +1.6; the others 0.237 each instead of 0.2265, +1.8 (the first behind a group of sums takes 0.32); waits 3.3 instead of 2.8, +0.5; sums 13.5 instead of 12.9, +0.5; the slow first matmuls +0.2; the two spreads 0.9 together instead of 1.8, -0.9. I had allowed for half rate only at the start. Nearly all of it is lost in half 0, which ends at 46.2. In the first trace there are seven slow matmuls more in such stretches and eight more at the start, and the end is 78.4. Behind PE's end the tables follow by 7.3 and 7.5 us, where the forecast had 7.2; both count from half 1's sums, as shown next.

Part 2's own sum came to the same 78 by errors that nearly cancel. DVE's waits up to the tables in the second trace:

```profile
DVE rv L265 <- PE chk L245: 7.2, 2, 4.7
DVE mu L296 <- DMA vecs<-in_vec_dram: 4.5, 1, 4.5
DVE hl L971 <- ACT hh L970: 4.1, 4, 1.8
DVE ev L1001 <- PE gm L1038: 1.5, 1, 1.5
```

With the small ones left out here they are 18.3 us, 13.8 of them behind `vecs`, where I had put "some 4 us of waits"; DVE's work is 63.6, not 70.1: the durations of the large operations come to the 51.5 that were summed, but each starts a little before the one ahead has ended, so that from start to start they take 45.7, and the small ones 18.0. So DVE did not set the tables by its work alone. Its rows in the second trace show where it stood:

```profile
41.35 1.06 DVE L1001 TENSOR_TENSOR ev<-gm,rbc 128x512 f32<-128x512 f32 x1 [1.47 <-PE gm L1038]
55.51 0.16 DVE L265 TENSOR_SCALAR rv<-chk 128x4 f32<-128x4 f32 x1 [4.74 <-PE chk L245]
...
75.26 2.94 DVE L1001 TENSOR_TENSOR ev<-gm,rbc 128x512 f32<-128x512 f32 x3
```

The wait for an eviction is half 0's; half 1's evictions wait for nothing. The last wait of any size is the one for half 1's sums, up to 55.51, and from 59.5 to the tables at 81.89 DVE has no idle time. So the tables come when PE has half 1's sums done plus what DVE has left to do then, 26.4 us. By Part 1's terms the sums would have been there at 51.5 (42.8, and 24 matmuls and four sums behind it), and with 26.4 the tables at 77.9: the 4 us by which half 1's sums were late are the 4 us of the tables. A delay on PE ahead of these sums, or more work on DVE behind them, reaches the tables. pair_sums has its sums 6.1 us sooner and 9.5 us more behind them; two_steps_again has its sums at 55.3 and 24.6 us behind them. half1_rooted is the exception, where DVE waits for PE once more at the end. Late tables then cost time at the end, as before_tables_late shows.

**Wrong, second: the last term of Part 4, "the 4.1 us of filler done early are missing as cover where RWKV starts", from 0 to 4.1, taken at 1.5.** The stage from S5's last outputs to RWKV's second group does not get shorter with PE's work in it. It took 50.8 us in the kernel before and 51.4 to 54.2 in all the others, with 274 PE records in it or 294 (tab20). In the second trace the 3.8 us of work done early came back whole as idle time, and 2.0 more. That this stage is longer in every trace than in the one of the kernel before is measured; why is not settled. With more filler done early one eviction less stands ahead of RWKV's setup on DVE, and PE's wait behind it is 3.7 to 4.1 in the traces of the change instead of 1.9; but tab20, where it is 1.9 again, has the longest stage. Late S5 outputs alone go with some of it (before_tables_late, 52.0), yet evict_plain has early outputs and 53.5. With one trace of the kernel before, its 50.8 may also be at the short end of what that kernel does. Nor did this stage set the time alone: early_roots and evict_two_steps are 6 to 7 us late at its end and 2 us or less at the program's. Nor does the place of the tables alone give the time: evict_two_steps and the change's second trace have S at 82.0 and 81.9, and ratios of 0.9998 and 1.0050.

The two terms are 3.8 and 4.6 of the 7.9 us by which the sum is off (-0.5 comes from the batches between). For the first the runs show the way it takes; for the second they show that the stage grew, and the cause stays open.

**The rivals.** *Slower* had the right sign and the wrong cause: the parameters landed early. What it said of any delay ahead of the tables, "goes one to one to the scans", held in the change's three traces (74.8 to 75.3 us from the tables to the first L616, 74.8 in the sum), not in the versions with another order (64.8 in tab20); the delay was PE's longer half 0 and DVE's wait for the sums behind it. *Faster* needed tables at 71; evict_plain, which has the plain evictions of that rival, had them at 74.9 and was level all the same, so its 7.6 us find no support here. *PE starts no earlier than 11* and *the second batch keeps its waits* did not occur in the change. Of the marks set beforehand, the tables at 82 to 86 lay outside 76 to 80, PE's end outside 70 to 71, and L610's end, at 156.6 and 160.4, later than 153 by about as much as the tables; the others were met or missed by little (a wait of 9.0 to 9.3 at L616 instead of 10, the rest of it at L546).
